# Down projection of a SwiGLU layer: three instead of two of four weight pieces by Strassen's seven products, in four pairs of blocks

## The chip, the cores and the metric

The kernel runs on one core of a Trainium2 chip. The metric is the time of one execution on the device, in microseconds (us). Five engines work side by side, each through its own queue in order: TensorE (PE in the rows; its weight loads are PEld), VectorE (DVE), ScalarE (ACT), GpSimd (POOL) and SyncE (SP), which here only issues transfers. They wait for each other through semaphores.

## The reference

One decoder layer with 256 positions and a model width of 2048. A token mixer with three branches comes first, then a feed-forward sublayer; each is followed by a layer norm. The change is in the feed-forward sublayer:

```
def swiglu_ffn(x, w_gu, w_down):
    gate, up = jnp.split(x @ w_gu, 2, axis=-1)
    return (jax.nn.silu(gate) * up) @ w_down
...
        x = layer_norm(ALPHA * x + swiglu_ffn(x, w_gu[l], w_down[l]), ln2_g[l], ln2_b[l])
```

`w_gu` is 2048 x 11264 and `w_down` 5632 x 2048, all float32.

## The kernel before

Every weight is cut into **pieces** of 256 rows x 512 columns (a tile of 128 partitions x 1024 floats, 512 KB). A list `pieces`, 632 long, holds them in the order in which TensorE uses them. Float32 accuracy comes from splitting each operand into a high half that TensorE takes as it is (ScalarE copies it, `wh`) and a low half (VectorE subtracts, `wl = raw - wh`), and from three products: high x high, high x low, low x high.

For each piece `i` the main loop issues, in this order: loads that have a free `raw` buffer (`load`, on SyncE's queue); the splits of later pieces (`split` is ScalarE's part and runs one piece further ahead than `split_lo`, VectorE's part, which stands three pieces ahead of the multiplications); the multiplications of piece `i` (`mults`); one entry of the list `later`; and, after a job's last piece, its evacuation (`job.evac`). That is also the order in each engine's queue. So what `split_lo` issues for piece `i + 3` stands ahead of the evacuation of a job that ends with piece `i`. Buffers come from rings: `raw` has 6, `wh` 5, `wl` 4.

The feed-forward sublayer has 11 blocks of 512 hidden columns. A block is a gate job and an up job of 8 pieces each (form "A"; TensorE's output is the hidden activation, transposed). `ev_ffgate` and `ev_ffup` take the sums out of PSUM and put the product `silu(gate) * up` into `S["hT", b, 0]` and `S["hT", b, 1]`, 256 hidden columns each. From block 2 on, `weave` puts a **down job** of four pieces into each gate or up job, one piece after every second piece of it: two blocks b0 and b0 + 1 that are already done are multiplied by one 512-column stripe j of `w_down`. There are 18 such woven jobs, for b0 = 0, 2, 4, 6 (four stripes each) and 8 (two stripes); what is left follows at the end as plain jobs.

Within a woven job two pieces are **plain**: `mul_b` makes 12 multiplications with 512 moving columns (2 halves of the positions x 2 halves of the rows x 3 products). The other two, k = 1 and 2, are Strassen pieces: `mul_seven` treats the piece as a 2 x 2 product of blocks, made with 7 block products instead of 8, so 21 multiplications with 256 moving columns. Strassen needs sums of weight blocks and of activations. The weight sums are made in `split_lo`: VectorE adds (L1145 to L1147), subtracts the low halves (L1148 and twice L204), and ScalarE copies the two high halves of the sums (L203); they go into a tile `s`, alternately in the slots "h0" and "s5". The activations' sums are made in `sums` inside `ev_ffup` (L896 to L903) for odd blocks; even blocks get a plain split.

The seven products are summed in the job's accumulator `ab` (two banks of PSUM) and in two more banks `c` and `d`, which come from a pool of two (tag "tr"). `ev_seven` (L933 to L944) adds `ab`, `c` and `d` into the result on VectorE, after ScalarE has copied `d` (L937). The next woven job can write its first Strassen piece only when those two banks are free again. The order of a job's four pieces is `(0, 2, 3, 1)`: k = 0 and k = 3 are plain.

Of the kernel before, what the change touches and what calls it, by code (L numbers as in the profile page):

```python
# [12 lines left out]
F32R = mybir.dt.float32r  # L13
I32 = mybir.dt.int32
AF = mybir.ActivationFunctionType
ALU = mybir.AluOpType
# [3 lines left out]
P = 128  # L20
NT = 2
T = 256
KT = D // P
DFF = 5632
NB = DFF // 512
H = 4
ALPHA = 2.0 ** 0.25
EPS = 1e-5
RAW_BUFS = 6
HL_BUFS = 4  # L30
SPLIT_AHEAD = 3
LOAD_AHEAD = 8
# [73 lines left out]
def layer_kernel(ctx: ExitStack, tc: tile.TileContext, xT_d, mem_d, memT_d, wi_d, wif_d, wkv_d,  # L106
                 wpa_d, wpb_d, wpc_d, wout_d, wgu_d, wdn_d, pp_d, bif_d, gws_d, gbs_d, bin_d, gln_d, xr_d, lnp_d, out_d):
    nc = tc.nc
    ve, ac, te, gp, sy = nc.vector, nc.scalar, nc.tensor, nc.gpsimd, nc.sync
# [4 lines left out]
    wp = ctx.enter_context(tc.tile_pool(name="wp", bufs=HL_BUFS))  # L114
# [7 lines left out]
    def nm(s):  # L122
        cnt[0] += 1
        return f"{s}{cnt[0]}"

    def slot(tag, shape, dt=F32):
        return big.tile(shape, dt, tag=tag, name=nm(tag))
# [126 lines left out]
    S = {}  # L254
# [370 lines left out]
    def once(key, make):  # L625
        if key not in S:
            S[key] = make()
        return S[key]
# [243 lines left out]

    later = []

    def ev_ffup(b):
        def f(job, hf):
            g = S["hid", b][:, 2 * hf:2 * hf + 2]
            odd = b % 2
            if hf == 0:
                if odd:  # L880
                    h = slot(("s3", "s1")[b // 2 % 2], [P, 2, 2, 8, P], F32R)
                else:
                    h = slot(("s6", "s6b")[b // 2 % 2], [P, 2, 2, 2, T], F32R)
                for i in range(2):
                    S["hT", b, i] = h[:, i]
            h = S["hT", b, hf]
            u = two(t2())
            comb(job, hf, u)
            ve.tensor_mul(g, g, u)
            if h.shape[2] != 8:  # L890
                later.append(lambda: split_from(g, h[:, :, 0], h[:, :, 1]))
                return
            a = flat(g).rearrange("p (a b) -> p a b", a=4)

            def sums():
                ac.activation(h[:, 0, 0:4], a, AF.Copy)  # L896
                s = t2([P, 4, P])
                ve.tensor_tensor(s[:, 0:2], a[:, 1:2].to_broadcast([P, 2, P]), a[:, 0:4:3], ALU.subtract)
                ve.tensor_sub(s[:, 2], a[:, 0], s[:, 1])
                ve.tensor_sub(s[:, 3], a[:, 2], s[:, 2])  # L900
                ac.activation(h[:, 0, 4:8], s, AF.Copy)
                ve.tensor_sub(h[:, 1, 0:4], a, h[:, 0, 0:4])
                later.insert(0, lambda: ve.tensor_sub(h[:, 1, 4:8], s, h[:, 0, 4:8]))  # L903

            later.append(sums)
        return halves(f)
# [21 lines left out]
    def ev_seven(j, first):  # L928
        def f(job):
            a = S["acc"][:, :, j * 512:(j + 1) * 512]  # L930
            ab, (c, d) = job.ps[0], job.cd
            if first:
                ve.scalar_tensor_tensor(a, a, ALPHA, ab, ALU.mult, ALU.add)  # L933
            else:
                ve.tensor_add(a, a, ab)
            e = t2()
            ac.activation(e, d, AF.Copy)  # L937
            w, z = t2(), t2([P, 2, T])
            ve.tensor_sub(w[:, 0:T], c[:, 0:T], e[:, 0:T])
            ve.tensor_sub(w[:, T:], w[:, 0:T], e[:, T:])  # L940
            ve.tensor_tensor(z, c[:, T:].unsqueeze(1).to_broadcast([P, 2, T]), two(w), ALU.subtract)
            ve.tensor_add(a[:, 0, T:], a[:, 0, T:], c[:, 0:T])
            ve.tensor_add(a[:, 1, T:], a[:, 1, T:], w[:, T:])
            ve.tensor_add(a[:, :, 0:T], a[:, :, 0:T], z)  # L944
        return f
# [115 lines left out]

    def weave(up, b0, j):

        act = lambda: Hid([S["hT", b0, 0], S["hT", b0 + 1, 0], S["hT", b0 + 1, 1], S["hT", b0, 1]])
        src = [wdn_d[j, 2 * b0 + i] for i in (0, 2, 3, 1)]
        dn = Job("B", src, act, 4, ev_seven(j, b0 == 0), seven=(1, 2))
        for k in range(8):
            pieces.append((up, k))
            if k % 2 == 1:
                pieces.append((dn, k // 2))  # L1070
# [14 lines left out]
    raw, hl, owned, cur, n7 = {}, {}, {}, [0], [0]  # L1085
# [3 lines left out]
    def load(i):  # L1089
        job, k = pieces[i]  # L1090
        r = wp.tile([P, 1024], F32, tag="raw", name=nm("raw"), bufs=RAW_BUFS)
        raw[i] = r
# [13 lines left out]
    def split(i):  # L1106
        job, k = pieces[i]
        r = raw[i]
        if k in job.own:
            tag, m = job.own[k]  # L1110
            if m == 0:
                S["own"] = slot(tag, [P, 2, 2, 1024], F32R)
            h = S["own"][:, m, 0]
            owned[i] = S["own"][:, m, 1]
        else:
            h = wp.tile([P, 1024], F32R, tag="wh", name=nm("wh"), bufs=HL_BUFS + 1)
        if k in job.seven:
            ac.activation(h[:, T:], r[:, T:], AF.Copy)  # L1118
        else:
            ac.activation(h, r, AF.Copy)  # L1120
        hl[i] = [h, None]

    def split0():
        r = raw.pop(0)
        h = wp.tile([P, 1024], F32R, tag="wh", name=nm("wh"), bufs=HL_BUFS + 1)
        l = wp.tile([P, 1024], F32R, tag="wl", name=nm("wl"))
        hl[0] = [h, l]
        for j in range(2):
            o = slice(j * 512, (j + 1) * 512)
            split_from(xraw[:, j], xT.one(j, 0), xT.one(j, 1))  # L1130
            split_from(r[:, o], h[:, o], l[:, o])

    def split_lo(i):
        l = owned.pop(i) if i in owned else wp.tile([P, 1024], F32R, tag="wl", name=nm("wl"))
        r = raw.pop(i)
        hl[i][1] = l
        job, k = pieces[i]
        if k not in job.seven:
            ve.tensor_sub(l, r, hl[i][0])  # L1139
            return  # L1140
        n7[0] += 1
        s = slot(("h0", "s5")[n7[0] % 2], [P, 2, 1024], F32R)
        hl[i].append(s)
        p, q = bc2(), bc2()
        ve.tensor_tensor(two(p), r[:, 0:T].unsqueeze(1).to_broadcast([P, 2, T]), two(r[:, T:3 * T]), ALU.add)  # L1145
        ve.tensor_add(q[:, 0:T], p[:, 0:T], r[:, 2 * T:3 * T])
        ve.tensor_add(q[:, T:], q[:, 0:T], r[:, 3 * T:])  # L1147
        ve.tensor_sub(l[:, T:], r[:, T:], hl[i][0][:, T:])  # L1148
        split_from(p, s[:, 0, 0:512], s[:, 1, 0:512])
        split_from(q, s[:, 0, 512:], s[:, 1, 512:])  # L1150
# [6 lines left out]
    def mul_b(job, k, h, l, t, half=None):  # L1157
        a = job.act()
        o, n = 0, 512
        if job.split and t == 1:  # L1160
            if half is None:
                mul_b(job, k, h, l, t, 0)
                mul_b(job, k, h, l, t, 1)
                return
            if job.ps[1] is None:
                job.ps[1] = [bank(), bank()]
            ps = job.ps[1][half][:, 0:T]
            o, n = half * T, T
        elif job.banks:
            if job.ps[t] is None:  # L1170
                job.ps[t] = bank()
            ps = job.ps[t]
        else:
            ps = acc(job, 0)[:, t]
        for j in range(2):
            kt = 2 * k + j
            wh, wl = h[:, j * 512 + o:j * 512 + o + n], l[:, j * 512 + o:j * 512 + o + n]
            f, e = k == 0 and j == 0, k == job.n - 1 and j == 1
            te.matmul(ps, a.sta(kt, 0, t), wh, start=f, stop=False)  # L1179
            te.matmul(ps, a.sta(kt, 0, t), wl, start=False, stop=False)  # L1180
            te.matmul(ps, a.sta(kt, 1, t), wh, start=False, stop=e)  # L1181

    def mul_seven(job, k, h, l, s):

        a = job.act().pairs[k]
        ab = acc(job, 0)
        first = job.cd is None
        if first:
            job.cd = [bank(), bank()]
        c, d = job.cd  # L1190
        end = k == job.seven[-1]
        w = lambda i: (h[:, i * T:(i + 1) * T], l[:, i * T:(i + 1) * T])
        u = lambda i: (s[:, 0, i * T:(i + 1) * T], s[:, 1, i * T:(i + 1) * T])

        def prod(out, i, b, start=False, stop=False):
            te.matmul(out, a[:, 0, i], b[0], start=start, stop=False)  # L1196
            te.matmul(out, a[:, 0, i], b[1], start=False, stop=False)  # L1197
            te.matmul(out, a[:, 1, i], b[0], start=False, stop=stop)  # L1198

        prod(c[:, 0:T], 0, w(1), start=first)  # L1200
        prod(ab[:, 0, T:], 2, w(3))
        prod(ab[:, 0, 0:T], 7, w(2))
        prod(c[:, T:], 5, u(0), stop=end)
        prod(d[:, T:], 4, u(1), start=first)
        prod(d[:, 0:T], 6, u(2), stop=end)
        prod(ab[:, 1, T:], 3, u(3))

    def mul_a(job, k, h, l, hf, w, j):
        a, kt = job.act(), 2 * k + j
# [80 lines left out]
    for i in range(N):  # L1290
        job, k = pieces[i]
# [79 lines left out]
```

## Time and profile before

| | |
|---|---|
| median of three runs | 1840.7 us (1840.7 to 1840.88) |
| the profiled execution's own time | 1840.85 us |
| its span, from first to last instruction | 1839.1 us |
| mean granted TensorE clock | 0.998 |
| TensorE busy | 1823.3 us, 99% of the span |
| VectorE / ScalarE busy | 1283.1 us (70%) / 945.9 us (51%) |
| data moved | 352.64 MB, mean 192 GB/s |

The shares are averages over the whole span. The woven stage alone, from 1187 to 1784 us, is nine blocks of about 66.3 us each.

In the rows a line starts with the start time in us and the duration in us, then the engine, the source line, the operation, and output <- inputs with their sizes; xN merges N equal instructions that follow each other, and the duration is then that of all N. A bracket at the end is idle time of the engine before the instruction and who ended it. A TensorE row's duration overlaps with the next one, so the pace of multiplications is read from the differences of their starts.

### The profile page before, as it was taken

The page shows a single profiled execution, that of the slowest core. Times are in us where ns is not written, and L with a number is a line of the kernel's source. Part 1 is how long each engine was busy: PE and PEld are TensorE (multiplying, and loading weights), DVE is VectorE, ACT ScalarE, POOL GpSimd, SP SyncE. Part 2 cuts the span into 40 slices and gives each one's busy share as a digit, 9 for nine tenths or more (in the row PEclk, how much of TensorE's full clock was granted, in tenths as well). Part 3 has the DMA queues.
Part 4 walks back from the last instruction along what each step waited for, and adds up shares of the span by engine and source line. Part 5 has one row for each costly group of instructions (what it writes and reads, how often), then busy time and mean ns, then how long its engine had stood idle before and what let it go on. Part 6 is the DMA issues. An engine that isn't in the chain of part 4 may idle for free.

```text
span 1839.1 us, 26103 instructions
## 1 busy us (share of the span) xinstructions
PE 1823.3 (99%) x10154; PEld 1575.3 (86%) x10154; DVE 1283.1 (70%) x1741; ACT 945.9 (51%) x1147; POOL 9.5 (1%) x24
## 2 busy tenths in 40 slices
PE   9999999999999999999999999999999999999997
PEld 8888888888888888888888888888888888888886
DVE  6886566557667666565555568577877878878787
ACT  6554465555555555544444355455555555555453
POOL 0000000000000000000000000000000000000001
PEclk9999999999999999999999999999999999999999
DMA  9666555555555555655556645665565565566656
GB/s 373 216 223 189 182 171 165 181 166 189 163 188 162 176 191 164 185 186 169 190 189 239 243 158 172 189 200 184 171 219 171 185 217 181 184 196 197 194 173 182
DMA packets 97627, 352.64 MB, mean 192 GB/s; under 512 B 10848, under 2 KB 11360, under 8 KB 96352
## 3 DMA queue, kind: packets, MB, share of 16 engines
q1 hardware_dynamic: 96496, 348.89, 58.5%
q0 software_dynamic: 576, 1.05, 0.5%
q8 instruction: 79, 1.29, 0.3%
q10 hardware_dynamic: 432, 1.05, 0.2%
q14 instruction: 44, 0.36, 0.1%
HBM read 348.85 MB, written 3.15 MB: 191 GB/s over the span
## 4 chain that ended last, share of the span: by engine, by line
PE 97%; DVE 2%; ACT 0%; DMA 0%; issue 0%; SPq 0%; DVEq 0%; ACTq 0%
PE acc L1214 45%; PE acc L1216 23%; PE acc L1181 7%; PE acc L1180 7%; PE acc L1179 7%; PE tr L1198 1%; PE tr L1196 1%; PE tr L1197 1%; PE acc L1198 1%; PE acc L1197 1%; PE acc L1196 1%; DVE wl L1139 1%; PE tr L198 1%; PE tr L199 0%; PE tr L200 0%; DVE t L841 0%
## 5 line engine op out<-in xcount | busy, mean ns | idle before, releaser
L1214 PE MATMUL acc<-s,wh 128*128 128x512 f32 x3520 | 966.2, 396 | 2.5 <-DVE s L846 1.1
L1139 DVE TENSOR_TENSOR wl<-raw,wh 128x1024 fp32r<-128x1024 f32 x589 | 712.3, 1222 | 362.8 <-PE acc L1216 180.9
L1120 ACT ACTIVATE wh<-raw 128x1024 fp32r<-128x1024 f32 x589 | 618.9, 1058 | 566.0 <-PE acc L1214 344.9
L1214 PEld LDWEIGHTS acc<-s,wh 128*128 128x128 f32 x3520 | 602.5, 188 | 86.6 <-DVE s L846 1.4
L1216 PEld LDWEIGHTS acc<-s,wl 128*128 128x128 f32 x3520 | 542.2, 189 | 80.9 <-DVE wl L1139 0.5
L1216 PE MATMUL acc<-s,wl 128*128 128x256 f32 x3520 | 560.8, 281 | 0.1
L1181 PE MATMUL acc<-wh,s 128*128 128x512 f32 x452 | 179.4, 397 | 0.0
L1179 PE MATMUL acc<-wh,s 128*128 128x512 f32 x452 | 179.0, 396 | 0.0
L1180 PE MATMUL acc<-wl,s 128*128 128x512 f32 x452 | 178.2, 394 | 0.0
L1181 PEld LDWEIGHTS acc<-wh,s 128*128 128x128 f32 x452 | 84.9, 188 | 20.4
L1180 PEld LDWEIGHTS acc<-wl,s 128*128 128x128 f32 x452 | 84.9, 188 | 19.4
L1179 PEld LDWEIGHTS acc<-wh,s 128*128 128x128 f32 x452 | 85.0, 188 | 18.6
L616 DVE TENSOR_TENSOR g<-g,acc 128x512 f32<-128x512 f32 x54 | 37.2, 688 | 50.3 <-ACT g L615 34.6
L615 ACT ACTIVATE g<-acc,pp 128x256 f32<-128x256 f32 x64 | 26.9, 472 | 28.9 <-PE acc L1216 28.9
L1118 ACT ACTIVATE wh<-raw 128x768 fp32r<-128x768 f32 x36 | 30.4, 845 | 18.4 <-PE acc L1214 11.7
L1181 PE MATMUL acc<-wh,s6b 128*128 128x512 f32 x96 | 38.1, 397 | 0.0
L1180 PE MATMUL acc<-wl,s6b 128*128 128x512 f32 x96 | 38.0, 396 | 0.0
L1179 PE MATMUL acc<-wh,s6b 128*128 128x512 f32 x96 | 37.8, 394 | 0.0
L612 ACT ACTIVATE t<-acc 128x512 f32<-128x512 f32 x38 | 22.7, 598 | 27.3 <-PE acc L1216 27.3
L616 DVE TENSOR_TENSOR t<-t,acc 128x512 f32<-128x512 f32 x38 | 26.1, 686 | 13.7 <-ACT t L612 13.7
L1148 DVE TENSOR_TENSOR wl<-raw,wh 128x768 fp32r<-128x768 f32 x36 | 34.3, 953 | 0.8
L203 ACT ACTIVATE s<-bc 128x512 fp32r<-128x512 f32 x36 | 22.8, 633 | 19.3 <-DVE bc L1145 15.2
(336 smaller groups left out, 1505.0 us busy)
## 6 DMA issues: line engine op xcount, KB each, us to landing
raw<-in_wi SPq DMA_DIRECT2D x238, 512.0 KB, 3.7
raw<-in_wgu SPq DMA_DIRECT2D x176, 512.0 KB, 4.2
raw<-in_wdn SPq DMA_DIRECT2D x88, 512.0 KB, 3.8
raw<-in_wkv SPq DMA_DIRECT2D x32, 512.0 KB, 3.6
raw<-in_wpb SPq DMA_DIRECT2D x32, 512.0 KB, 4.4
raw<-in_wout SPq DMA_DIRECT2D x32, 512.0 KB, 3.6
raw<-in_wpa SPq DMA_DIRECT2D x16, 512.0 KB, 3.6
raw<-in_wpc SPq DMA_DIRECT2D x16, 512.0 KB, 3.6
```

Of the source, the lines that this page charges most:

```text
L616: ve.tensor_add(out, out, ps[:, :, 0:T])
L1120: ac.activation(h, r, AF.Copy)
L1139: ve.tensor_sub(l, r, hl[i][0])
L1148: ve.tensor_sub(l[:, T:], r[:, T:], hl[i][0][:, T:])
L1179: te.matmul(ps, a.sta(kt, 0, t), wh, start=f, stop=False)
L1180: te.matmul(ps, a.sta(kt, 0, t), wl, start=False, stop=False)
L1181: te.matmul(ps, a.sta(kt, 1, t), wh, start=False, stop=e)
L1196: te.matmul(out, a[:, 0, i], b[0], start=start, stop=False)
L1197: te.matmul(out, a[:, 0, i], b[1], start=False, stop=False)
L1198: te.matmul(out, a[:, 1, i], b[0], start=False, stop=stop)
L1214: te.matmul(ps, w[:, o:o + P], a.both(kt), start=k == 0 and j == 0, stop=False)
L1216: te.matmul(ps[:, 0:T], w[:, o:o + P], a.hi(kt), start=False, stop=k == job.n - 1 and j == 1)
```

## The change

1. In the 14 woven jobs with b0 = 2, 4, 6 and 8, three pieces of four are Strassen pieces: k = 0, 1, 2. The order of the pieces becomes `(1, 2, 3, 0)`, so that `S["hT", b0, 0]` is the one plain piece and comes last. The four jobs with b0 = 0 stay as they were.
2. For the even blocks 2, 4, 6 and 8, the second half `S["hT", b, 1]` gets the Strassen form (the function `sums`). The first half moves into a new tile `lot` in slot "s5", which also holds every second `s` tile.
3. The plain piece's low half in these 14 jobs is no longer subtracted on VectorE. In `split`, ScalarE writes `-wh` into `wl`, and a transfer that GpSimd issues adds the weights from HBM to it (`gp.dma_start(..., accum_op=ALU.add)`). The `raw` buffer of that piece is free after ScalarE's copy.
4. `raw` has 5 buffers instead of 6, `wl` 5 instead of 4.
5. In `mul_seven` the first products into `ab` begin the accumulation when the Strassen piece is the job's first; in the plain piece one multiplication with 512 columns in each half of the rows j = 0 becomes two with 256.

```diff
-RAW_BUFS = 6
+RAW_BUFS = 5
...
+    def lot():
+        return once("lot", lambda: slot("s5", [P, 4096], F32R))
+
     def ev_ffup(b):
         def f(job, hf):
             g = S["hid", b][:, 2 * hf:2 * hf + 2]
-            odd = b % 2
+            q = b // 2 % 2
             if hf == 0:
-                if odd:
-                    h = slot(("s3", "s1")[b // 2 % 2], [P, 2, 2, 8, P], F32R)
+                if b % 2:
+                    h = slot(("s3", "s1")[q], [P, 2, 2, 8, P], F32R)
+                    hs = h[:, 0], h[:, 1]
+                elif b in (0, NB - 1):
+                    h = slot(("s6", "s6b")[q], [P, 2, 2, 2, T], F32R)
+                    hs = h[:, 0], h[:, 1]
                 else:
-                    h = slot(("s6", "s6b")[b // 2 % 2], [P, 2, 2, 2, T], F32R)
+                    h = slot(("s6", "s6b")[q], [P, 2, 8, P], F32R)
+                    o = (2 + q) * 1024
+                    hs = lot()[:, o:o + 1024].rearrange("p (k a t) -> p k a t", k=2, a=2), h
                 for i in range(2):
-                    S["hT", b, i] = h[:, i]
+                    S["hT", b, i] = hs[i]
...
-        act = lambda: Hid([S["hT", b0, 0], S["hT", b0 + 1, 0], S["hT", b0 + 1, 1], S["hT", b0, 1]])
-        src = [wdn_d[j, 2 * b0 + i] for i in (0, 2, 3, 1)]
-        dn = Job("B", src, act, 4, ev_seven(j, b0 == 0), seven=(1, 2))
+        o, seven = ((0, 2, 3, 1), (1, 2)) if b0 == 0 else ((1, 2, 3, 0), (0, 1, 2))
+        act = lambda: Hid([S["hT", b0 + i // 2, i % 2] for i in o])
+        src = [wdn_d[j, 2 * b0 + i] for i in o]
+        dn = Job("B", src, act, 4, ev_seven(j, b0 == 0), seven=seven)
...
         hl[i] = [h, None]
+        if 0 in job.seven and k not in job.seven:
+            l = wp.tile([P, 1024], F32R, tag="wl", name=nm("wl"), bufs=HL_BUFS + 1)
+            ac.activation(l, h, AF.Identity, scale=-1.0)
+            gp.dma_start(l, job.src[k], accum_op=ALU.add)
+            raw.pop(i)
+            hl[i][1] = l
...
     def split_lo(i):
-        l = owned.pop(i) if i in owned else wp.tile([P, 1024], F32R, tag="wl", name=nm("wl"))
+        if hl[i][1] is not None:
+            return
+        l = owned.pop(i) if i in owned else wp.tile([P, 1024], F32R, tag="wl", name=nm("wl"), bufs=HL_BUFS + 1)
...
-        s = slot(("h0", "s5")[n7[0] % 2], [P, 2, 1024], F32R)
+        if n7[0] % 2:
+            s = lot()[:, 0:2048].rearrange("p (a b) -> p a b", a=2)
+        else:
+            s = slot("h0", [P, 2, 1024], F32R)
...
-            te.matmul(ps, a.sta(kt, 0, t), wh, start=f, stop=False)
+            if 0 in job.seven and t == 1 and j == 0:
+                for x in (0, T):
+                    te.matmul(ps[:, x:x + T], a.sta(kt, 0, t), wh[:, x:x + T], start=False, stop=False)
+            else:
+                te.matmul(ps, a.sta(kt, 0, t), wh, start=f, stop=False)
...
-        first = job.cd is None
+        first, lead = job.cd is None, k == 0
...
-        prod(ab[:, 0, T:], 2, w(3))
+        prod(ab[:, 0, T:], 2, w(3), start=lead)
...
-        prod(ab[:, 1, T:], 3, u(3))
+        prod(ab[:, 1, T:], 3, u(3), start=lead)
```

The program's order of instructions shows what these lines do on the engines. Line numbers of the changed kernel differ: L1157 is the old L1139, L1166 to L1169 the old L1145 to L1148, L907 to L912 the old L898 to L903, L944 to L953 the old L935 to L944.

**First place: VectorE, at the end of the up job of block 5, where a down job ends and the next gate job is to begin.** The first row takes the last half of the up job's result out, the last row begins the evacuation of the down job. Before:

```order
L889 TENSOR_TENSOR g_13819<-g_13819,t_14132 128x512
L1139 TENSOR_TENSOR wl_14140<-raw_14012,wh_14107 128x1024
L898 TENSOR_TENSOR t_14155<-g_13819 128x256
L899 TENSOR_TENSOR t_14155<-g_13819,t_14155 128x128
L900 TENSOR_TENSOR t_14155<-g_13819,t_14155 128x128
L902 TENSOR_TENSOR s_14127<-g_13819,s_14127 128x512
L935 TENSOR_TENSOR s_8705<-s_8705,acc_13916 128x2x512
```

and now:

```order
L898 TENSOR_TENSOR g_13969<-g_13969,t_14302 128x512
L1166 TENSOR_TENSOR bc_14309<-raw_14185 128x512
L1167 TENSOR_TENSOR bc_14310<-bc_14309,raw_14185 128x256
L1168 TENSOR_TENSOR bc_14310<-bc_14310,raw_14185 128x256
L1169 TENSOR_TENSOR wl_14308<-raw_14185,wh_14275 128x768
L204 TENSOR_TENSOR s_10448<-bc_14309,s_10448 128x512
L204 TENSOR_TENSOR s_10448<-bc_14310,s_10448 128x512
L907 TENSOR_TENSOR t_14335<-g_13969 128x256
L908 TENSOR_TENSOR t_14335<-g_13969,t_14335 128x128
L909 TENSOR_TENSOR t_14335<-g_13969,t_14335 128x128
L911 TENSOR_TENSOR s_14297<-g_13969,s_14297 128x512
L944 TENSOR_TENSOR s_8705<-s_8705,acc_14076 128x2x512
```

The one plain subtraction for the next job's first down piece (L1139) has become the six instructions of a Strassen piece (L1166 to L204). They stand ahead of the activations' sums and of the evacuation.

**Second place: VectorE, after the up job of the even block 6, two gate pieces later, up to the split of the next job's second down piece (k = 1).** Before:

```order
L1139 TENSOR_TENSOR wl_13548<-raw_13411,wh_13515 128x1024
L204 TENSOR_TENSOR s6b_13504<-g_13196,s6b_13504 128x2x256
L1139 TENSOR_TENSOR wl_13574<-raw_13433,wh_13546 128x1024
L1145 TENSOR_TENSOR bc_13598<-raw_13460 128x512
L1146 TENSOR_TENSOR bc_13599<-bc_13598,raw_13460 128x256
L1147 TENSOR_TENSOR bc_13599<-bc_13599,raw_13460 128x256
L1148 TENSOR_TENSOR wl_13596<-raw_13460,wh_13572 128x768
```

and now:

```order
L1157 TENSOR_TENSOR wl_13681<-raw_13542,wh_13638 128x1024
L907 TENSOR_TENSOR t_13704<-g_13301 128x256
L908 TENSOR_TENSOR t_13704<-g_13301,t_13704 128x128
L909 TENSOR_TENSOR t_13704<-g_13301,t_13704 128x128
L911 TENSOR_TENSOR s6b_13629<-g_13301,s6b_13629 128x512
L1157 TENSOR_TENSOR wl_13712<-raw_13562,wh_13679 128x1024
L912 TENSOR_TENSOR s6b_13629<-t_13704,s6b_13629 128x512
L1166 TENSOR_TENSOR bc_13737<-raw_13589 128x512
L1167 TENSOR_TENSOR bc_13738<-bc_13737,raw_13589 128x256
L1168 TENSOR_TENSOR bc_13738<-bc_13738,raw_13589 128x256
L1169 TENSOR_TENSOR wl_13735<-raw_13589,wh_13710 128x768
```

The even block's second half has got the sums that odd blocks had already: five instructions (L907 to L912) in place of one (L204).

**Third place: ScalarE, in a gate job of the woven stage, around the job's plain piece (k = 3).** The rows begin with the copies of the third down piece's weight sums (L203). Before:

```order
L203 ACTIVATE h_13670<-bc_13671 128x512
L203 ACTIVATE h_13670<-bc_13672 128x512
L1120 ACTIVATE wh_13706<-raw_13592 128x1024
L1120 ACTIVATE wh_13728<-raw_13621 128x1024
L1120 ACTIVATE wh_13750<-raw_13643 128x1024
```

and now:

```order
L203 ACTIVATE s_10448<-bc_13820 128x512
L203 ACTIVATE s_10448<-bc_13821 128x512
L1130 ACTIVATE wh_13853<-raw_13747 128x1024
L1130 ACTIVATE wh_13875<-raw_13777 128x1024
L1134 ACTIVATE wl_13877<-wh_13875 128x1024
L1130 ACTIVATE wh_13900<-raw_13799 128x1024
```

One row is new, the copy of `-wh` into `wl` (L1134). GpSimd's queue, which held nothing in this stage, now has one transfer behind each of them, 14 in all.

## Rows read from the trace of the kernel before

**Rows 1.** Window of one block: length, busy time per engine, clock, DMA share, GB/s.

```profile
1452.10:1518.30 66.20, 66.20 (x389) 58.27 (x388) 53.53 (x75) 35.26 (x44) 0.00 (x0) 1.00 0.59 191
```

**Rows 2.** Timeline of TensorE, block 5: plain piece, gate pieces, Strassen piece, gate piece.

```profile
1391.41 0.39 PE L1179 MATMUL acc<-wh,s6b 128*128 128x512 f32 x1
...
1394.21 1.08 PE L1214 MATMUL acc<-s,wh 128*128 128x512 f32 x4
...
1399.83 0.28 PE L1196 MATMUL tr<-wh,s 128*128 128x256 f32 x1
1399.95 0.28 PE L1197 MATMUL tr<-wl,s 128*128 128x256 f32 x1
...
1402.34 1.09 PE L1214 MATMUL acc<-s,wh 128*128 128x512 f32 x4
```

**Rows 3.** Timeline of VectorE, end of block 5 and start of block 6.

```profile
1446.69 1.22 DVE L1139 TENSOR_TENSOR wl<-raw,wh 128x1024 fp32r<-128x1024 f32 x1 [2.96 <-issue]
...
1451.42 1.22 DVE L1139 TENSOR_TENSOR wl<-raw,wh 128x1024 fp32r<-128x1024 f32 x1
1452.55 0.42 DVE L898 TENSOR_TENSOR t<-g 128x256 f32<-128x256 f32 x1
...
1456.79 0.41 DVE L942 TENSOR_TENSOR s<-s,tr 128x256 f32<-128x256 f32 x1
...
1460.93 0.42 DVE L898 TENSOR_TENSOR t<-g 128x256 f32<-128x256 f32 x1
...
1462.52 0.68 DVE L1145 TENSOR_TENSOR bc<-raw 128x512 f32<-128x512 f32 x1
...
1464.04 0.95 DVE L1148 TENSOR_TENSOR wl<-raw,wh 128x768 fp32r<-128x768 f32 x1
...
1466.12 0.68 DVE L903 TENSOR_TENSOR s<-t,s 128x512 fp32r<-128x512 f32 x1
```

**Rows 4.** Timeline of TensorE, blocks 5 and 6: first up and gate pieces, down pieces.

```profile
1418.93 1.08 PE L1214 MATMUL acc<-s,wh 128*128 128x512 f32 x4
...
1452.06 1.08 PE L1214 MATMUL acc<-s,wh 128*128 128x512 f32 x4
...
1466.21 0.28 PE L1197 MATMUL tr<-wl,s 128*128 128x256 f32 x1
...
1482.62 0.40 PE L1180 MATMUL acc<-wl,s 128*128 128x512 f32 x1
```

**Rows 5.** Timeline of VectorE, start of block 5 (block 4 is even).

```profile
1391.94 0.69 DVE L204 TENSOR_TENSOR s<-g,s 128x512 fp32r<-128x512 f32 x1
1392.54 1.22 DVE L1139 TENSOR_TENSOR wl<-raw,wh 128x1024 fp32r<-128x1024 f32 x1
...
1395.20 0.95 DVE L1148 TENSOR_TENSOR wl<-raw,wh 128x768 fp32r<-128x768 f32 x1
```

**Rows 6.** Timeline of VectorE, end of block 5's gate job.

```profile
1417.56 1.22 DVE L1139 TENSOR_TENSOR wl<-raw,wh 128x1024 fp32r<-128x1024 f32 x1
1419.13 1.22 DVE L935 TENSOR_TENSOR s<-s,acc 128x1024 f32<-128x1024 f32 x1 [0.35 <-PE acc L1181]
...
1421.79 0.41 DVE L942 TENSOR_TENSOR s<-s,tr 128x256 f32<-128x256 f32 x1
```

**Rows 7.** Timeline of ScalarE, gate jobs of blocks 5 and 6, before the plain piece.

```profile
1404.93 1.06 ACT L1120 ACTIVATE wh<-raw 128x1024 fp32r<-128x1024 f32 x1 [2.15 <-issue]
...
1469.70 0.64 ACT L203 ACTIVATE h<-bc 128x512 fp32r<-128x512 f32 x1 [2.27 <-DVE bc L1145]
...
1471.17 1.99 ACT L1120 ACTIVATE wh<-raw 128x1024 fp32r<-128x1024 f32 x2
```

**Rows 8.** DMA issues: output <- input, queue, count, KB each, median us to landing.

```profile
raw<-in_wdn SPq DMA_DIRECT2D x88, 512.0 KB, 3.8
...
out_y<-s POOLq DMA_DIRECT2D x4, 256.0 KB, 5.1
out_y<-s SPq DMA_DIRECT2D x4, 256.0 KB, 2.4
```

More of the change, by code (lines that the diff above doesn't have):

```diff
@@ L1125, in split0 @@
         h = wp.tile([P, 1024], F32R, tag="wh", name=nm("wh"), bufs=HL_BUFS + 1)
-        l = wp.tile([P, 1024], F32R, tag="wl", name=nm("wl"))
+        l = wp.tile([P, 1024], F32R, tag="wl", name=nm("wl"), bufs=HL_BUFS + 1)
         hl[0] = [h, l]
```

## The prediction

> **What bounds the kernel now.** I read the table by window first, over one block of the woven stage [rows 1]: of 66.20 us TensorE is busy 66.20, at the full granted clock, VectorE 53.53, ScalarE 35.26, and the transfers take 0.59 of the DMA engines. So TensorE's columns set the pace, and each multiplication saved shortens the stage as long as nothing else arrives late. Then TensorE's timeline, for the price of a piece: a plain piece takes 1394.21 - 1391.41 = 2.80 us, two gate pieces 1399.83 - 1394.21 = 5.62, a Strassen piece 1402.34 - 1399.83 = 2.51 [rows 2]. A Strassen piece's multiplications run at 2.51 / 21 = 0.120 us each, with their weight loads hidden.
>
> VectorE's 53.53 of 66.20 us looks like room, but it isn't spread evenly, so the third view was its timeline where one down job ends and the next begins. Before the end of an up job VectorE idles (2.96 us ahead of the row at 1446.69); from 1451.42 on it runs without a gap through the activations' sums, the evacuation and the next splits [rows 3]. Its last result before TensorE wants it is the low half of the second down piece, done at 1464.04 + 0.95 = 1464.99. TensorE first reads it in the piece's second multiplication, at 1466.21 [rows 4]. The slack there is 1.22 us. After an even block the same result is done at 1395.20 + 0.95 = 1396.15 [rows 5] and used at 1399.95 [rows 2]: slack 3.80.
>
> **The change, part by part.**
>
> *TensorE.* In 14 jobs one plain piece becomes a Strassen piece: 14 x (2.80 - 2.51) = 4.06 us less. The one multiplication of 512 columns that becomes two of 256 costs 2 x 0.120 - 2.80 / 12 = 0.007 us a job, nothing. The changed start flags cost nothing.
>
> *VectorE at the end of an odd block (3, 5, 7, 9; four times).* The next job's first down piece is now a Strassen piece, so one subtraction of 1452.55 - 1451.42 = 1.13 us becomes the six-instruction split of 1466.12 - 1462.52 = 3.60 us [rows 3], ahead of the sums and the evacuation in VectorE's queue: 2.47 us more, in a stretch that had no gap. It waits behind the up job's evacuation, which TensorE itself releases, so it can't start earlier. Two things are then late. First, the bank for `d`. The program's waits show that the banks change places: `c` of the new job takes the one that ScalarE's copy frees, `d` takes the one that L942 frees. L942 ended at 1456.79 + 0.41 = 1457.20 and will end at 1459.67; TensorE wants `d` after two gate pieces and 12 multiplications, at 1452.06 + 5.62 + 1.43 = 1459.11 [rows 4]. That is a wait of 0.56 us. Second, the low half of the second down piece: ready at 1464.99 + 2.47 = 1467.46, wanted at 1466.21 - 0.29 = 1465.92. That is 1.54 us, and it contains the first wait, since both come from one queue that is 2.47 us late. Four times: 6.16 us.
>
> *VectorE at the end of an even block (4, 6, 8; three times).* The same 2.47 us, and the even block's second half now has sums: 1462.52 - 1460.93 = 1.59 us [rows 3] in place of one subtraction of 1392.54 - 1391.94 = 0.60 [rows 5], and one more subtraction of that size: 1.59 more. Ready at 1396.15 + 2.47 + 1.59 = 1400.21, wanted at 1399.95 - 0.29 = 1399.66: 0.55 us, three times, 1.65 us. The bank for `d` is in time here, as no sums stand ahead of L942.
>
> *VectorE at the end of a gate job (seven times).* There VectorE had 0.35 us to spare before the evacuation [rows 6]. With the long split it starts at 1417.56 + 3.60 = 1421.16 instead of 1419.13, and L942 ends 2.03 later, at 1424.23; `d` is wanted at 1418.93 + 5.62 + 1.43 = 1425.98 [rows 4]. Cost 0, with 1.75 us of cover; if that were gone, each us would cost 7.
>
> *VectorE's saved subtraction* for the plain piece (1.13 us) stood before the up job's end, where VectorE idles anyway. It is worth nothing.
>
> *The accumulating transfer.* ScalarE's second copy (1.06 us) and the transfer must both be done before TensorE's second multiplication of the plain piece. In a gate job after an odd block the copy of the high half ended at 1471.17 + 1.99 = 1473.16 [rows 7]; `-wh` would be done at 1474.22, and TensorE wanted the low half at 1482.62 [rows 4], 8.40 later. The changed kernel takes 2.47 of that, since ScalarE's queue waits there for VectorE's sums (2.27 us idle in the row), and gives back 1.54 - 0.29 = 1.25: 7.2 us are left, in four jobs. In block 5 the copy ends at 1405.99, so `-wh` at 1407.05, against 1482.62 - 66.3 = 1416.3: 9.3, in the seven up jobs and, less what the backlog takes, in the other three. No transfer of this kind and size is in the trace. Floor: 5.1 us, that of half the bytes [rows 8]. Ceiling: that row doubled, 10.2, which doubles its fixed part too. I take the load of the same size, 3.8, and add what the accumulating one of 256 KB has over the plain one, 5.1 - 2.4 = 2.7: 6.5 us, under 7.2. Cost 0. It adds 14 x 512 KB to a stage whose DMA engines are 0.59 busy.
>
> *Five raw buffers.* A load is issued one piece (2.8 us) later. It lands after 3.8 us, and ScalarE's copy runs four pieces, some 11 us, ahead of TensorE. Cost 0; the bound is 2.8 us once, at the start, where loads queue longest. The fifth `wl` buffer removes waits of VectorE on TensorE that nothing waits for: 0.
>
> **The sum.** -4.06 + 6.16 + 1.65 = +3.75 us on the profiled execution's 1840.85, which stands 0.15 above the median: 1844.45, rounded to 1844.5. I count 0.2%, 3.7 us, as about what a measurement of this kernel can tell from no change: 1837.0 to 1844.4 is "within".
>
> **Rivals.**
>
> *The transfer is late (0.23).* At 8.2 us it makes TensorE wait 1.0 in the four tight jobs and up to 1.0 in three more: 4 to 7 us on top, 1848.5 to 1851.5; at the ceiling 25 us and more. For it: four landings that were measured with little other traffic, and loads on the same engines. Against: an accumulation into SBUF needn't read back from HBM. The Trainium skill ("DMA: Bandwidth & Descriptors", Anatomy of one DMA) gives about 2.0 us plus bytes at 436 GB/s for GpSimd's transfers; an estimate by it is 3.2 us here and would take this rival away. For the 256 KB row it would be 2.6 us, where the trace has 5.1, so I don't lean on it.
>
> *VectorE isn't late (0.10), faster.* The place is the same boundary. If the subtraction saved on the plain piece let VectorE begin its backlog earlier, by 1.54 us or more, no wait would reach TensorE at either kind of block: 1840.7 - 4.1 = 1836.6. Against: the idle 2.96 us ahead of the boundary show that VectorE has nothing that it may start sooner.
>
> *Only the bank delays TensorE (0.08).* If the low half came in time after all (by VectorE's queue being shorter than I add up past the evacuation), what is left is the wait for `d`, 4 x 0.56: 1840.7 - 4.06 + 2.24 = 1838.9. The Trainium skill ("Perfetto Trace Analysis", Optimization Strategy) reads the same gap repeated on the engine that should be saturated as too few SBUF or PSUM buffers; by that rule the two banks are the whole cause. The rows put VectorE's arrival later than the bank's, so I keep it as a rival.
>
> *Something else makes it slower (0.07):* ScalarE, with 14 more copies, late with the copy of `d`; or loads late with five buffers. 1847 to 1852.
>
> **How the numbers follow.** The forecast has 0.52, between 1842 and 1847: a few tenths either way at seven boundaries. The likeliest time is 1844.5. Faster by over 0.2%: 0.10, the second rival. Within 0.2%: the third rival's 0.08 and a little under half of the forecast, 0.35. Slower: 0.55. The range leaves out the faster rival below and the transfer's long tail above: 1838.5 to 1850.
>
> **What would show it.** Strassen pieces of 2.5 us at k = 0, 1, 2 show the gain. Right: TensorE idle by about 0.5 us before the first `d` product and 1.0 more in the second down piece of blocks 4, 6, 8, 10, with VectorE named as the releaser; about 0.5 in 5, 7, 9; blocks of 66.3 - 0.6 = 65.7 us plus these waits. Wrong: no idle time there; or idle time at the plain piece, ended by the transfer, whose landing would then be over 7 us after its issue.

## The result and the profile after

The changed kernel takes 1872.68 us (median of four runs, 1871.89 to 1875.97); the kernel before took 1840.75 beside it (four runs). The ratio is 1.0176, 95% interval 1.0163 to 1.0189: 31.9 us slower, far outside the predicted 1838.5 to 1850. The direction was forecast, the size was not.

The profiled execution took 1872.43 us. From the page of the changed kernel, the line of busy times, the DMA queues (packets, MB, share of the 16 engines over the span) and the chain that ended last:

```profile
PE 1830.5 (98%) x10294; PEld 1584.5 (85%) x10294; DVE 1299.8 (69%) x1813; ACT 972.8 (52%) x1193; POOL 20.4 (1%) x38
...
q1 hardware_dynamic: 96496, 348.89, 56.0%
q0 software_dynamic: 2592, 8.39, 2.7%
...
PE 84%; DVE 9%; DMA 5%; ACT 1%; issue 1%; ACTq 0%; DVEq 0%; SPq 0%
```

A transfer now stands on the chain. The window of block 6, the same block as in [rows 1], from its first gate piece to about that of block 7, with the same columns (length, busy time of TensorE, its weight loads, VectorE, ScalarE and GpSimd, granted clock, DMA share, GB/s):

```profile
1458.80:1530.10 71.30, 68.08 (x409) 60.15 (x408) 56.06 (x83) 38.60 (x49) 1.71 (x2) 0.98 0.62 192
```

The window is 71.3 us long instead of 66.2, and TensorE is idle in 3.2 of it. What it waited for, over the whole kernel (the three largest entries; us in total, times, longest):

```profile
PE acc L1205 <- DMA wl<-in_wdn: 18.6, 8, 3.5
PE tr L1222 <- DVE wl L1169: 3.8, 7, 0.7
PE tr L1221 <- DVE s L951: 1.7, 4, 0.5
```

The two lower entries are the waits that the prediction worked out for VectorE, 4 and 7 times. The upper one is the rival that it gave 0.23. TensorE's timeline at the start of block 6, from its first gate piece, with the first two down pieces of its gate job:

```profile
1458.79 1.10 PE L1239 MATMUL acc<-s,wh 128*128 128x512 f32 x4
...
1464.43 0.28 PE L1221 MATMUL tr<-wh,s 128*128 128x256 f32 x1
...
1466.45 0.39 PE L1221 MATMUL tr<-s,s 128*128 128x256 f32 x1 [0.43 <-DVE s L951]
1466.67 0.28 PE L1222 MATMUL tr<-s,s 128*128 128x256 f32 x1
...
1467.63 1.09 PE L1239 MATMUL acc<-s,wh 128*128 128x512 f32 x4
...
1473.33 0.28 PE L1221 MATMUL tr<-wh,s 128*128 128x256 f32 x1
...
1474.24 0.38 PE L1222 MATMUL tr<-wl,s 128*128 128x256 f32 x1 [0.64 <-DVE wl L1169]
...
1476.72 0.63 PE L1239 MATMUL acc<-s,wh 128*128 128x512 f32 x2
```

The two Strassen pieces take 1467.63 - 1464.43 = 3.20 and 1476.72 - 1473.33 = 3.39 us instead of 2.51 [rows 2]. The rows of VectorE that ended these waits:

```profile
1465.98 0.41 DVE L951 TENSOR_TENSOR s<-s,tr 128x256 f32<-128x256 f32 x1
...
1473.23 0.95 DVE L1169 TENSOR_TENSOR wl<-raw,wh 128x768 fp32r<-128x768 f32 x1
```

L951 ends 1466.39 - 1458.79 = 7.60 us after the block's first gate piece; the prediction put it at 1459.67 - 1452.06 = 7.61. The low half ends 15.39 after it; predicted, 1467.46 - 1452.06 = 15.40.

Now the plain piece of the same job. GpSimd's issue of the transfer, then TensorE's timeline:

```profile
1483.74 0.85 POOL L1135 DMA_DIRECT2D wl<-in_wdn  x1 [35.65 <-PE acc L1223]
```

```profile
1490.51 0.40 PE L1204 MATMUL acc<-wh,s 128*128 128x512 f32 x1
1493.05 0.53 PE L1205 MATMUL acc<-wl,s 128*128 128x512 f32 x1 [2.14 <-DMA wl<-in_wdn]
1493.39 0.61 PE L1206 MATMUL acc<-wh,s 128*128 128x512 f32 x1
1493.80 0.63 PE L1204 MATMUL acc<-wh,s 128*128 128x512 f32 x1
...
1496.79 0.40 PE L1205 MATMUL acc<-wl,s 128*128 128x512 f32 x1
...
1497.26 0.63 PE L1239 MATMUL acc<-s,wh 128*128 128x512 f32 x2
```

TensorE wants the low half at 1490.51 + 0.23 = 1490.74, 7.0 us after the issue, and goes on 9.31 us after it. The multiplications that follow start 0.43 us apart instead of 0.23, until 1496.8; so the whole piece takes 1497.26 - 1490.51 = 6.75 us instead of the 2.81 of such a piece that isn't held up: the wait costs 2.3 us and the slow stretch 6.75 - 2.81 - 2.3 = 1.6 more. The same reading for all transfers that were late, in us from the issue ("gate 4" is the down job woven into the gate job of block 4):

| job | wanted | TensorE goes on | late |
|---|---|---|---|
| gate 4 | 6.99 | 9.93 | 2.94 |
| gate 5 | 6.60 | 8.76 | 2.16 |
| gate 6 | 7.00 | 9.31 | 2.31 |
| gate 7 | 7.61 | 9.79 | 2.18 |
| gate 8 | 7.02 | 10.68 | 3.66 |
| gate 9 | 7.62 | 10.44 | 2.82 |
| gate 10 | 6.65 | 9.87 | 3.22 |
| up 10 | 8.98 | 9.60 | 0.62 |

That is 19.9 us of lateness (the view of waits counts 18.6, since the tail of the row before counts as busy). The slow stretches after the stops in gate 6, 8 and 10 add 1.6, 2.7 and 1.4 us, together 5.7; the granted clock in each is 0.50. The other six up jobs had 8.96 to 8.98 us as well, and their transfers were in time.

### The profile page after: what moved, and what is told of

It reads as the page before. It is cut to its first block, busy times and chain, and to the rows that moved or that the text cites. A ratio compares the mean times of both kernels' runs of the same rounds, so it can differ in the third digit from the quotient of the medians.

```text
span 1870.7 us, 26363 instructions
## 1 busy us (share of the span) xinstructions
PE 1830.5 (98%) x10294; PEld 1584.5 (85%) x10294; DVE 1299.8 (69%) x1813; ACT 972.8 (52%) x1193; POOL 20.4 (1%) x38
## 4 chain that ended last, share of the span: by engine, by line
PE 84%; DVE 9%; DMA 5%; ACT 1%; issue 1%; ACTq 0%; DVEq 0%; SPq 0%
PE acc L1239 38%; PE acc L1241 20%; PE acc L1205 6%; PE acc L1206 6%; PE acc L1204 6%; DMA wl<-in_wdn 4%; DVE wl L1157 2%; PE tr L1222 1%; PE tr L1223 1%; PE tr L1221 1%; DVE s L204 1%; PE acc L1223 1%; PE acc L1221 1%; PE acc L1222 1%; DVE wl L1169 1%
## 5 line engine op out<-in xcount | busy, mean ns | idle before, releaser
L1130 ACT ACTIVATE wh<-raw 128x1024 fp32r<-128x1024 f32 x575 | 602.3, 1055 | 506.3 <-PE acc L1239 284.9
L1157 DVE TENSOR_TENSOR wl<-raw,wh 128x1024 fp32r<-128x1024 f32 x561 | 672.4, 1220 | 189.5 <-ACT wh L1130 175.9
L1205 PE MATMUL acc<-wl,s 128*128 128x512 f32 x460 | 184.5, 401 | 18.6 <-DMA wl<-in_wdn 18.6
L1206 PE MATMUL acc<-wh,s 128*128 128x512 f32 x460 | 184.4, 401 | 0.0
L1204 PE MATMUL acc<-wh,s 128*128 128x512 f32 x446 | 177.8, 399 | 0.0
L1128 ACT ACTIVATE wh<-raw 128x768 fp32r<-128x768 f32 x50 | 42.1, 842 | 50.4 <-PE acc L1239 47.5
L203 ACT ACTIVATE s<-bc 128x512 fp32r<-128x512 f32 x50 | 31.7, 633 | 36.1 <-DVE bc L1166 28.9
L1169 DVE TENSOR_TENSOR wl<-raw,wh 128x768 fp32r<-128x768 f32 x50 | 47.6, 951 | 0.0
L204 DVE TENSOR_TENSOR h<-bc,h 128x512 fp32r<-128x512 f32 x50 | 32.3, 687 | 6.0 <-ACT h L203 6.0
L1166 DVE TENSOR_TENSOR bc<-raw 128x512 f32<-128x512 f32 x50 | 34.2, 684 | 0.0
L204 DVE TENSOR_TENSOR s<-bc,s 128x512 fp32r<-128x512 f32 x50 | 32.1, 684 | 0.0
```

Source lines behind the costliest of these rows:

```text
L204: ve.tensor_sub(lo_ap, src, hi_ap)
```

## Experiments

**The change without the transfer.** The plain piece's low half goes back to VectorE.

```diff
-        if 0 in job.seven and k not in job.seven:
-            l = wp.tile([P, 1024], F32R, tag="wl", name=nm("wl"), bufs=HL_BUFS + 1)
-            ac.activation(l, h, AF.Identity, scale=-1.0)
-            gp.dma_start(l, job.src[k], accum_op=ALU.add)
-            raw.pop(i)
-            hl[i][1] = l
```

> The changed kernel, but the plain piece's low half is subtracted on VectorE as before: no second ScalarE copy, no accumulating transfer; raw keeps 5 buffers. Theory A, the late transfer: in the changed kernel TensorE waited 18.6 us for the transfer and 5.5 us for VectorE, and three stretches at half clock followed such waits; without the transfer only the Strassen gain and the VectorE waits are left: 1840.75 - 4.06 + 5.5 = 1842.2 us, no wait for a transfer, full clock. Rival B, the third Strassen piece or the fifth raw buffer itself costs the time (loads later, TensorE's clock falling for another reason): the time stays over 1855 us.

Measured: 1846.21 us beside 1840.55, ratio 1.003 (1.0019 to 1.0041), clock 0.998. Its two largest waits:

```profile
PE tr L1216 <- DVE wl L1163: 3.7, 7, 0.7
PE tr L1215 <- DVE s L951: 1.7, 4, 0.4
```

Rival B falls: the third Strassen piece, five buffers and the clock cost nothing like 30 us by themselves. The transfer is worth 1872.68 - 1846.21 = 26.5 us. But 1846.2 isn't the 1842.2 that was expected, because that sum took two sizes wrongly. TensorE's timeline of this run, from one plain piece to the next with no stop between them:

```profile
1418.06 0.39 PE L1198 MATMUL acc<-wh,s 128*128 128x512 f32 x1
...
1420.87 1.10 PE L1233 MATMUL acc<-s,wh 128*128 128x512 f32 x4
...
1426.51 0.28 PE L1215 MATMUL tr<-wh,s6b 128*128 128x256 f32 x1
...
1450.95 0.39 PE L1198 MATMUL acc<-wh,s 128*128 128x512 f32 x1
```

A job that isn't held up takes 1450.95 - 1418.06 = 32.89 us instead of 1452.06 - 1418.93 = 33.13 [rows 4]. The plain piece, with 13 multiplications instead of 12, takes 2.81 us, and all four pairs of gate or up pieces take 5.64, where before two of four took 5.62. So the gain is 14 x 0.24 = 3.4 and not 4.06. And the held pieces lose 1.66 at an odd boundary and 0.65 at an even one, 4 x 1.66 + 3 x 0.65 = 8.6, where the view of waits counts only 5.4. After each of these stops the first multiplication is followed after 0.22 us instead of 0.12, as at 1466.45 in the rows above, and the rest is the tail of the row before the stop, which counts as busy. 8.6 - 3.4 = 5.2, measured 5.7.

**The transfer without the change.** The kernel before, with two Strassen pieces and its order of pieces, and with the transfer for the last plain piece; it also has the change's five `raw` and five `wl` buffers:

```diff
...
+        if job.seven and k == 3 and job.xf:
+            l = wp.tile([P, 1024], F32R, tag="wl", name=nm("wl"), bufs=HL_BUFS + 1)
+            ac.activation(l, h, AF.Identity, scale=-1.0)
+            gp.dma_start(l, job.src[k], accum_op=ALU.add)
...
+        dn.xf = b0 > 0
...
```

> The kernel before with the one thing added that theory A blames: in the 14 jobs with b0 = 2 to 8 the last plain piece's low half comes by ScalarE's negative copy and the accumulating transfer; two Strassen pieces and the order of pieces stay, raw has 5 buffers, wl 5. VectorE has no backlog here, so the transfer is issued some 8.4 to 9.3 us before TensorE wants it. Theory A1, the transfer's own length: it lands after 8.7 to 10.6 us in the gate jobs as in the changed kernel, and TensorE waits 0.3 to 2 us in most of seven jobs: 1844 to 1855 us. Theory A2, the backlog on VectorE pushes the loads of the raw buffers together and the transfer shares the DMA engines with five of them: here the loads are spread, it lands after 7 to 8.4 us everywhere, no wait: 1840 to 1842 us.

Measured: 1849.54 us beside 1840.55, ratio 1.0051 (1.0035 to 1.0066). TensorE's largest wait, and the transfer's landing over all 14 issues:

```profile
PE acc L1189 <- DMA wl<-in_wdn: 7.5, 6, 1.7
```

```profile
DMA to landing us min/median/max: 6.3/8.7/10.1
```

A2, as put, falls: VectorE has no backlog here, and the gate jobs still land at 8.7 to 10.1 us. Here TensorE wants the data about 8.1 us after the issue in gate jobs after an odd block and about 9.0 in all others. Without any backlog the transfer, with the five `raw` buffers, costs 9 us. That the loads are spread out here, as A2 supposed, isn't borne out: by their issues, three or four are in flight when a gate job's transfer is issued; in the changed kernel it is three.

**A plain write instead of the accumulation**, which leaves the weight itself in the low half.

```diff
-            gp.dma_start(l, job.src[k], accum_op=ALU.add)
+            gp.dma_start(l, job.src[k])
```

> The changed kernel, but GpSimd's transfer writes instead of accumulating: the plain piece's low half is then the whole weight, so the products with it are not the reference's. Bytes, queue and time of issue are the same. Theory A1, the addition on arrival is what makes it long: landing falls to 6.5 us or less, the waits of TensorE for it vanish, 1841.5 to 1845 us. Theory A2, sharing the DMA engines with the loads in flight: landing stays 8.5 to 10.5 us in the gate jobs, 1862 to 1873 us.

Measured: 1851.93 us beside 1840.55 (1849.81 to 1853.72), ratio 1.0061 (1.0047 to 1.0075); TensorE waits 2.4 us for it. The landing here, and then in the changed kernel:

```profile
DMA to landing us min/median/max: 6.1/7.1/7.8
```

```profile
DMA to landing us min/median/max: 6.8/9.0/10.6
```

The transfers' packets, MB and share of the DMA engines from 1321 to 1780 us (13 transfers), in the same order:

```profile
q0 software_dynamic: 1872, 6.82, 4.2%
```

```profile
q0 software_dynamic: 1872, 6.82, 8.4%
```

The packets of the same bytes take 4.2% x 459 / 13 = 1.5 us of all 16 engines written and 3.0 us accumulated, and the accumulated ones land 1.9 us later. In the run with the plain write, loads and GpSimd's transfers of the same size landed as follows (count, KB each, median us to landing, from 1321 to 1780 us):

```profile
raw<-in_wgu SPq DMA_DIRECT2D x107, 512.0 KB, 4.5
raw<-in_wdn SPq DMA_DIRECT2D x59, 512.0 KB, 4.4
wl<-in_wdn POOLq DMA_DIRECT2D x13, 512.0 KB, 7.2
```

So a write that GpSimd issues lands about 2.7 us after a load of the same size before anything is added. Neither theory is the whole: the addition has a price, but even the plain write lands later than the 6.5 us forecast for the accumulation.

**The low half wanted later.** In the changed kernel's plain piece the four products with `wl` come last.

```diff
...
+            if 0 in job.seven:
+                for t in range(NT):
+                    for j in range(2):
+                        te.matmul(acc(job, 0)[:, t], job.act().sta(2 * k + j, 0, t), l[:, j * 512:(j + 1) * 512],
+                                  start=False, stop=j == 1)
```

> The changed kernel, but in the plain piece TensorE makes the four products that need the transferred low half last: it wants it after eight multiplications (1.87 us) instead of after one (0.23), 1.64 us later; bytes, issue and landing stay. Theory A, the landings of 8.7 to 10.6 us against budgets of 6.6 to 7.6 us are the whole cost (26 us over the kernel without the transfer): each wait shrinks by 1.64, the eight that were 2.9, 2.1, 2.3, 2.1, 3.6, 2.8, 3.2 and 0.6 become 1.3, 0.5, 0.7, 0.5, 2.0, 1.2, 1.6 and 0, in sum 7.8, and the clock falls less often: 1854 us, up to 1858 with the falls. Rival, the transfer harms in another way (VectorE or loads slowed): over 1862 us.

Measured: 1857.5 us beside 1841.21 (1857.14 to 1858.03), clock 0.998, with the same VectorE waits as before and this wait for the transfer:

```profile
PE acc L1284 <- DMA wl<-in_wdn: 8.4, 7, 2.1
```

1.64 us more time take 15 us off: 8.4 us of waiting instead of 18.6, and the 5.7 us at the lower clock are gone. The landings stayed (median 9.1, longest 11.4). The transfer harms by being late, and in no other way that would show.

**Loads taken away.** The six pieces after each plain piece are not loaded but split from one constant tile; raw has 4 buffers to make room.

```diff
...
+        if 459 < i < 616 and 1 <= (i - 459) % 12 <= 6:
+            raw[i] = keep
+            return
...
```

> The changed kernel, but the six pieces that follow each plain piece of the first 13 such jobs are not loaded: they are split from one constant tile, so their products are not the reference's; raw has 4 buffers to make room for it. In the changed kernel exactly loads of these pieces are in flight during a transfer. Theory A2, sharing the DMA engines: the transfer alone lands after 5 to 6 us everywhere, TensorE doesn't wait for it, and gate and up jobs no longer differ. Theory A1, the transfer's own length: 8.5 us and more in the gate jobs still, TensorE waits 15 us or more.

Measured: the transfer lands after 7.0 to 9.6 us, median 8.1, and TensorE waits 18.1 us for it (one run, 1875.06 us). This didn't separate the theories as meant: later loads moved into the gap (by their issues, one to four overlapped each transfer), and with 4 raw buffers the transfer was issued only 5.2 to 5.9 us before it was wanted in the gate jobs. So ten of twelve pieces were left out (`<= 10` in the line above).

> As the kernel with six pieces not loaded, but ten of the twelve pieces between two plain pieces are not loaded (their products are not the reference's), so that the SyncE queue can run ahead and no load is in flight during a transfer. In the run with six pieces left out other loads moved into the gap, and the transfer still landed after 7.0 to 9.6 us; its packets then took 3.0 to 3.3 us of all 16 engines and began 3 us after its issue, while loads issued 1.4 us ahead of it were still on the engines. Theory A1, its own length: about 7 us even on empty engines. Theory A2, sharing: without loads it lands after 5 us, and TensorE's waits for it end.

> The same with a plain write instead of the accumulation (the plain piece's products are wrong as well). If the addition on arrival costs what the kernel with the plain write and all loads showed (landing 7.1 us in the median instead of 9.0; packets half as long), it lands 1.5 to 1.9 us earlier than in the run before; if that difference came from the loads' traffic, both land alike.

Measured, one run each: 1856.07 us with the accumulation, TensorE waits 5.4 us for it; 1849.23 with the plain write, 0.9. Landing with the accumulation, then with the plain write:

```profile
DMA to landing us min/median/max: 6.3/7.7/8.6
```

```profile
DMA to landing us min/median/max: 4.8/5.8/7.1
```

One or two loads still overlap most of the transfers here. With most of the traffic gone both land 1.3 us sooner (9.0 to 7.7, 7.1 to 5.8), and the difference between them stays 1.9. The two prices add: A1 and A2 each hold a part. In the first six up jobs, where the one or two loads beside the transfer were all issued before it, the accumulation lands at 6.3 to 7.4.

**The plain piece first.** If VectorE's waits come from the long split that stands ahead of the evacuation, another order of the pieces removes them, and no transfer is needed.

```diff
-        o, seven = ((0, 2, 3, 1), (1, 2)) if b0 == 0 else ((1, 2, 3, 0), (0, 1, 2))
+        o, seven = ((0, 2, 3, 1), (1, 2)) if b0 == 0 else ((0, 1, 2, 3), (1, 2, 3))
...
-        if 0 in job.seven and k not in job.seven:
...
-        prod(ab[:, 0, 0:T], 7, w(2))
+        prod(ab[:, 0, 0:T], 7, w(2), stop=k == 3)
...
-        prod(ab[:, 1, T:], 3, u(3), start=lead)
+        prod(ab[:, 1, T:], 3, u(3), start=lead, stop=k == 3)
```

> Three Strassen pieces as in the changed kernel, but in the order (0, 1, 2, 3): the plain piece is the first of the job and its low half is subtracted on VectorE, so that at the end of an up job VectorE has one subtraction ahead of the evacuation, as before, and the third long split comes in the middle of the job; no transfer; raw 5, wl 5. By the pace of the pieces in the kernel without the transfer a job of this kind is 32.87 us where it isn't held up, against 33.13 before: a gain of 14 x 0.26 = 3.6 us. Theory A, VectorE's waits (8.6 us by that kernel's pieces) come from the long split ahead of the evacuation: they vanish, 1840.6 - 3.6 = 1837.0 us. Rival, VectorE has no room for a third long split wherever it stands: TensorE waits 5 us or more elsewhere, 1841.5 us and over.

Measured: 1837.25 us beside 1841.21, ratio 0.9979 (0.997 to 0.9988): 4 us faster than the kernel before, small but clear of the noise, and 9 us faster than the change with its low half on VectorE. Its woven stage in one window, to be read as [rows 1]:

```profile
1187.00:1780.00 593.00, 593.00 (x3622) 528.94 (x3621) 505.10 (x716) 323.59 (x414) 0.00 (x0) 1.00 0.60 191
```

TensorE has no idle time in it. VectorE is busier than in the change as made (1313.2 us here against 1299.8, over the whole program), and in this stage TensorE waits for it nowhere. VectorE's timeline at the end of an odd block shows why:

```profile
1450.50 1.22 DVE L1151 TENSOR_TENSOR wl<-raw,wh 128x1024 fp32r<-128x1024 f32 x1
1451.63 0.42 DVE L907 TENSOR_TENSOR t<-g 128x256 f32<-128x256 f32 x1
...
1453.22 1.21 DVE L944 TENSOR_TENSOR s<-s,acc 128x1024 f32<-128x1024 f32 x1
```

One subtraction stands ahead of the sums and the evacuation, as in [rows 3], and not the six instructions of the long split; that split now stands in the middle of the job.

## Why the prediction was right and wrong

*TensorE's gain* held in kind. It was mis-sized: 3.4 us instead of 4.06, or 0.24 a job instead of 0.29. The sum took the gate and up pieces as unchanged; in the changed job two more pairs of them take 5.64 us instead of 5.62, and the plain piece takes 2.81 instead of 2.80.

*VectorE's backlog* held in place and size: odd boundaries 1.66 us each against 1.54, even 0.65 against 0.55, and none from a gate job to an up job. L951 and the low half ended within 0.01 us of the forecast. What the 7.81 lacked is TensorE's slower restart, about 0.1 us a boundary (at an odd one the second stop contains the first). Together gain and backlog make 5.2 us, where the forecast had 3.75. The kernel without the transfer shows them: 1846.21 us, inside the range. The third rival, the bank alone, and the second, VectorE in time, are out: both waits were there, and so was the time.

*The step that failed is the accumulating transfer:* "I take the load of the same size, 3.8, and add what the accumulating one of 256 KB has over the plain one, 5.1 - 2.4 = 2.7: 6.5 us, under 7.2. Cost 0." It took 8.7 to 10.6 us in the gate jobs, median 9.8. What failed is the 2.7. It came from four accumulations of half the bytes and into HBM, at the end of the kernel where little else moves, set against writes that SyncE issued. In the woven stage a plain write that GpSimd issues is already about 2.7 us slower than a load, and the addition puts 1.9 on top. The 6.5 is about what the quiet run shows in its up jobs; the stage's loads add to it. The first 4.0 us after an issue and the 5.9 that follow, in the changed kernel's block 4 (packets, MB, share of the engines by queue; q1 carries the loads, q0 the transfer):

```profile
q1 hardware_dynamic: 296, 1.09, 97.0%
```

```profile
q1 hardware_dynamic: 324, 1.18, 52.3%
q0 software_dynamic: 144, 0.52, 45.6%
```

In the first 4.0 us, in which no packet of the transfer moves, loads that were issued shortly before hold 97% of the engines; after that the two share them about half and half. By the records of the packets, the other transfers fit this: in the seven gate jobs three loads are in flight at the issue and the transfer's first packet comes 4.3 to 4.8 us after it; in the seven up jobs it is two loads and 2.7 to 3.4 us. That makes up most of the difference between the landings (median 9.8 and 7.8). It isn't shown as the cause: no run changes the number of loads alone, and with the plain write the two kinds of job differ less (first packet after 3.0 to 4.1 and 3.0 to 3.6 us).

The stage's mean of 0.59, which the prediction gave as the engines' load, hides that a transfer issued beside a burst of loads finds full engines. Why a write that GpSimd issues lands later than a load even in the quiet run (5.8 us) stays open. The Trainium skill ("DMA: Bandwidth & Descriptors", Issuing engines are not separate DMA queues) says that transfers from all issuing engines run on the same 16 DMA engines and interleave; the second of these windows, where both queues have packets, agrees. The same page's fit (Anatomy of one DMA), an estimate of 3.2 us, is missed by both quiet runs (5.8 written, 7.7 accumulated), as it was by the 256 KB row.

*The time it had* was short as well. In the four jobs at 7.2 by the sum it was 6.65 to 7.02: GpSimd issues the transfer 0.3 us after ScalarE's copy ends, which was left out. For the gate jobs of blocks 5, 7 and 9 the prediction gave "9.3 ... less what the backlog takes" and didn't work that out; it was 6.60 to 7.62, so seven jobs were tight and not four. With the other term right this alone would have cost 0: 6.5 is under all of them.

*The ceiling* was close: 10.2 us and "25 us and more" on top, against 9.8 in the gate jobs and 26.5. That the two totals are so near is partly luck: the forecast didn't have TensorE's clock after the stops, 5.7 of these 26, and six of seven up jobs, where a landing at 10.2 would have been late, had theirs in time. That the transfer's price had no row of its kind and size, while 25 us hung on it, should have widened the range to there.

The chance of "within", 0.35, is 0.08 and 0.27 of the forecast's 0.52; that is a little over half, not under.

The sum as measured: -3.4 + 8.6 + 19.9 + 5.7 = 30.8 us, and about 0.1 of restart after each of the five other stops for the transfer, 31.3 in all. The profiled executions differ by 1872.43 - 1840.85 = 31.6; 0.3 us are not assigned.

## What to carry to other kernels

Price a transfer by rows with its kind, its size and its neighbours: here the same 512 KB landed after 4.0 to 4.5 us as a load, 7.1 written by GpSimd, 9.0 accumulated, and the last two 1.3 sooner with most loads gone. When the time left is within a few us of such a price, the wait belongs in the range. And before work is taken off an engine with 70% busy time, see whether it can stand elsewhere in the engine's queue: VectorE had room for all of it in the middle of the job, and the order of four pieces was worth 9 us (1846.2 to 1837.3) with nothing taken off.

## What the runs showed of the hardware that was not expected

The packets of an accumulating transfer into SBUF took the DMA engines twice as long as those of a plain write of the same 512 KB: 3.0 against 1.5 us of all 16 (a load by SyncE: 54.0% x 459 / 157 = 1.6). GpSimd's instruction that issues it took 857 ns in the median instead of 528.

TensorE's granted clock fell after three of the stops and not after others. Windows of the changed kernel after the stop in gate 6 and after the longer one in gate 4:

```profile
1494.00:1496.00 2.00, 2.00 (x8) 1.61 (x7) 1.71 (x3) 1.59 (x4) 0.00 (x0) 0.50 0.51 119
1354.50:1357.00 2.50, 2.48 (x12) 2.06 (x13) 2.05 (x3) 1.93 (x4) 0.00 (x0) 1.00 0.65 197
```

0.50 is the lower of its two levels, 1.2 instead of 2.4 GHz. TensorE had been idle for 2.14 us ahead of the first window and for 2.78 us ahead of the second, where the clock stayed up. So the length of the last stop doesn't decide it alone; what else does stays open.
